# Stick-breaking attention weights turned in 32x32 squares on VectorE and gathered through DRAM

## The chip, the cores and the metric

The kernel runs on one core of one Trainium2 chip. The metric is device time in microseconds (us), the median of a few runs; a profile is one further execution, with its own time. Engines are named as in the profile: PE (TensorE matmul), PEld (its weight load), DVE (VectorE), ACT (ScalarE), POOL (GpSimd) and SP (SyncE, which only issues DMAs here).

## The reference

One decoder layer on 1024 tokens of width 1024, everything in float32:

```python
h = rms_norm(x, norm_gain) * (1 + scale) + shift              # scale, shift, gate from c
q, k, v, z_a, u, z_b, m_a, m_b = split(h @ w_in)              # 8 times 1024 columns
# stick-breaking attention, 16 heads of 64, strictly causal (mask: key < query)
z = q @ k.T * 64 ** -0.5
log_1m_beta = where(mask, -softplus(z), 0)
suffix = cumsum_from_the_right(log_1m_beta) - log_1m_beta
w = where(mask, exp(log_sigmoid(z) + suffix), 0)
attn = w @ v
p_a = (attn * silu(z_a)) @ w_branch_a
p_b = (causal_pooling(u) * silu(z_b)) @ w_branch_b
out = (sigmoid(m_a) * p_a + sigmoid(m_b) * p_b) @ w_out
y = rms_norm(x + gate * out, final_gain)
```

## The kernel before, in words

**Precision.** Operands of the large products are split into a high and a low float32r part, and a product is high*high + high*low + low*high: three matmuls of 128 rows and 512 columns. All matmuls and PE transposes are issued through one helper, so that they have one line, L92, and are told apart by their tiles.

**Stages.** The tokens are reversed on the host, so the causal mask keeps keys that come after the query, and the products of (1 - sigmoid) run from left to right. First come normalisation and the projection u (tiles `ua`, `u`), then v (`v`, stored to DRAM as `v_d`), then the pooling branch (`wzb`, `pool`, `pb`), then attention, and last the branch product (`pa`) and the output product (`o`).

**Attention.** The 16 heads form 8 pairs p of two heads h. Queries are taken in units (p, h, t): t is 0 to 3 and stands for two blocks of 128 queries, qb = 2t and 2t+1. Because of the mask a unit with t = 0 has 1024 and 896 keys, one with t = 3 only 256 and 128. A pair's units come in the order `HT_ORDER`: (h, t) = (0,0), (0,2), (1,0), (1,2), (0,1), (0,3), (1,1), (1,3). For a unit:

- `z_items` (L559 on): PE makes the logits in PSUM, in up to two chunks for a block (tile `z`, two PSUM banks). ACT writes two sigmoids of each chunk, `om` = sigmoid(-z/8) and `be` = sigmoid(z/8) (L576, L577). POOL sets the diagonal block's masked part to 1 and 0 (L581). DVE runs a product scan over `om` (L583) and multiplies `be` by it (L584): `be` is then the weight block, queries on partitions.
- `turn` (L591 on): for a pair kp of key blocks PE transposes up to four 128x128 squares of `be` against `ident` into one PSUM bank (`tr`, two banks); ACT copies the high part (L602, `wt`), DVE the low part (L603).
- `product`: PE multiplies `wt` with the values `vv` of the pair (tile `av`, two banks), and `finish` adds its parts (ACT L626, DVE L628, tile `tp`). After the second head POOL multiplies by the gate silu(z_a), kept in SBUF as `za` (L631), and SP stores the result to `ga_d` (L632).

**Projections as filler.** Between these PE runs the projections of k, q, z_a and of the gates m_a, m_b (tile `p`, two banks `pj`): 40 weight tiles of 16 quanta, a quantum being three 512-column matmuls. `use_k` and `use_q` evict with ACT and DVE (L488, L489; L481, L482), `use_za` with ACT and DVE (L497, L498), the gates with ACT.

**Order.** The attention stage is written as steps, eight to a pair. Step i makes the logits of the unit three places ahead (`LEAD`), turns chunks two ahead (`DEPTH`) of the product, multiplies unit i, and fills up with 70/8 quanta of projection. On PE this order is fixed by hand (`pinned`). The order on ACT, DVE, POOL and SP is chosen by the build's scheduler; each engine then executes its own list strictly in order. SP carries nearly all DMAs, in one queue.

**End.** `load_ga` (L541 on) reads `ga_d` back in 512-column pieces and splits them (ACT L549, DVE L550) into the operand of `pa`.

## Time and profile before

| what | value |
|---|---|
| median of 3 runs | 1249.1 us (1248.1 to 1249.2) |
| profiled execution, its own time | 1250.94 us |
| its span, first to last instruction | 1249.2 us |
| PE busy | 1215.2 us (97%) |
| DVE busy | 810.5 us (65%) |
| ACT busy | 546.3 us (44%) |
| POOL busy | 227.6 us (18%) |
| granted TensorE clock | 0.995 |
| attention stage, about 420 to 1066 us | PE 642.23, DVE 476.04, ACT 374.32 of 646 us |

Busy time is the time in which an engine executes. Every engine is in order, so an instruction that waits holds what is behind it. A line of a group reads: line, engine, operation, out<-in by tile names, shape, count | busy us, mean ns of one | idle time of the engine just before them and what ended it. A line of the timeline reads: start, duration, engine, line, operation, tiles, shape, count, and in brackets the idle time before it.

### The profile page before, as it was taken

The page shows a single profiled execution, that of the slowest core. Times are in us where ns is not written, and L with a number is a line of the kernel's source. Part 1 is how long each engine was busy: PE and PEld are TensorE (multiplying, and loading weights), DVE is VectorE, ACT ScalarE, POOL GpSimd, SP SyncE. Part 2 cuts the span into 40 slices and gives each one's busy share as a digit, 9 for nine tenths or more (in the row PEclk, how much of TensorE's full clock was granted, in tenths as well). Part 3 has the DMA queues.
Part 4 walks back from the last instruction along what each step waited for, and adds up shares of the span by engine and source line. Part 5 has one row for each costly group of instructions (what it writes and reads, how often), then busy time and mean ns, then how long its engine had stood idle before and what let it go on. Part 6 is the DMA issues. An engine that isn't in the chain of part 4 may idle for free.

```text
span 1249.2 us, 16044 instructions
## 1 busy us (share of the span) xinstructions
PE 1215.2 (97%) x5744; PEld 1005.2 (80%) x5744; DVE 810.5 (65%) x1085; ACT 546.3 (44%) x1022; POOL 227.6 (18%) x373
## 2 busy tenths in 40 slices
PE   4999999899999999999999999999999999999998
PEld 3888888688888888888888888888888888888886
DVE  6723452999511168786887877788796864685654
ACT  4654331321111256565566656566565654232101
POOL 2100010111112333221312222132222310001001
PEclk9999999989999999999999999999999999999999
DMA  8649994752344411232322333232233225985612
GB/s 325 265 151 345 320 371 163 274 202 93 118 144 135 151 52 50 69 127 90 105 89 94 114 110 111 73 121 89 89 119 110 74 89 186 352 287 170 201 65 85
DMA packets 72946, 192.97 MB, mean 154 GB/s; under 512 B 7713, under 2 KB 21025, under 8 KB 70946
## 3 DMA queue, kind: packets, MB, share of 16 engines
q1 hardware_dynamic: 62098, 172.80, 40.3%
q10 hardware_dynamic: 10768, 19.14, 4.6%
q8 instruction: 45, 0.74, 0.2%
q14 instruction: 35, 0.29, 0.1%
HBM read 137.38 MB, written 50.34 MB: 150 GB/s over the span
## 4 chain that ended last, share of the span: by engine, by line
PE 78%; DVE 10%; issue 5%; DMA 2%; POOL 1%; ACT 1%; POOLq 0%; SPq 0%; DVEq 0%; ACTq 0%
PE p L92 30%; PE pa L92 7%; PE pb L92 7%; PE v L92 7%; PE o L92 6%; PE av L92 4%; PE z L92 4%; PE u L92 4%; PE wt L92 4%; PE ua L92 2%; DVE om L583 1%; DVE be L584 1%; DMA l_raw<-in_w_in 1%; DVE win L393 1%; PE wzb L92 1%
## 5 line engine op out<-in xcount | busy, mean ns | idle before, releaser
L92 PE MATMUL p<-hT,w 128*128 128x512 f32 x1920 | 534.5, 399 | 0.0
L92 PEld LDWEIGHTS p<-hT,w 128*128 128x128 f32 x1920 | 341.5, 188 | 56.7 <-issue 0.5
L583 DVE TENSOR_TENSOR_SCAN om<-om 128x512 f32<-128x512 f32 (+7 forms) x128 | 175.2, 1368 | 51.7 <-POOL om L581 28.6
L576 ACT ACTIVATE om<-z 128x512 f32<-128x512 f32 (+2 forms) x192 | 94.3, 491 | 104.0 <-PE z L92 101.8
L603 DVE TENSOR_TENSOR wt<-wt,wt 128x512 fp32r<-128x512 f32 (+1 forms) x160 | 101.0, 632 | 47.3 <-ACT wt L602 46.0
L581 POOL TENSOR_SCALAR_AFFINE_SELECT om<-om 128x128 f32<-128x128 f32 x128 | 65.7, 514 | 328.1 <-ACT om L576 301.8
L602 ACT CAST wt<-wt 128x512 fp32r<-128x512 f32 (+1 forms) x160 | 87.3, 546 | 68.7 <-PE wt L92 65.2
L584 DVE TENSOR_TENSOR be<-be,om 128x511 f32<-128x511 f32 (+7 forms) x128 | 99.7, 779 | 10.8 <-ACT wt L602 0.5
L92 PE MATMUL av<-wt,vv 128*128 128x512 f32 x320 | 94.4, 376 | 0.0
L92 PEld LDWEIGHTS wt<-ident,be 128*128 128x128 f32 x576 | 72.0, 140 | 27.5 <-DVE wt L603 3.2
L577 ACT ACTIVATE be<-z 128x512 f32<-128x512 f32 (+2 forms) x192 | 93.6, 487 | 0.0
L92 PE MATMUL wzb<-hT,wzb 128*128 128x512 f32 x384 | 92.9, 398 | 0.1
L92 PE MATMUL wt<-ident,be 128*128 128x128 f32 x576 | 89.2, 273 | 3.8 <-DVE wt L603 3.8
L92 PE MATMUL o<-wo,mhl 128*128 128x512 f32 (+2 forms) x408 | 90.4, 380 | 0.0
L92 PE MATMUL pa<-ga,wa 128*128 128x512 f32 x384 | 89.8, 392 | 0.0
L92 PE MATMUL pb<-gb,wb 128*128 128x512 f32 x384 | 88.1, 391 | 0.0
L92 PEld LDWEIGHTS wzb<-hT,wzb 128*128 128x128 f32 x384 | 73.8, 192 | 16.8 <-DVE zs L411 0.5
L92 PE MATMUL v<-wv,hT 128*128 128x512 f32 x384 | 87.2, 389 | 0.0
L92 PEld LDWEIGHTS o<-wo,mhl 128*128 128x128 f32 x408 | 74.6, 188 | 14.4
L92 PEld LDWEIGHTS pa<-ga,wa 128*128 128x128 f32 x384 | 72.1, 188 | 15.9
L92 PEld LDWEIGHTS pb<-gb,wb 128*128 128x128 f32 x384 | 72.1, 188 | 15.8
L92 PEld LDWEIGHTS v<-wv,hT 128*128 128x128 f32 x384 | 72.1, 188 | 14.9
(121 smaller groups left out, 1458.4 us busy)
## 6 DMA issues: line engine op xcount, KB each, us to landing
w_raw<-in_w_in SPq DMA_DIRECT2D x40, 512.0 KB, 4.3
l_raw<-in_w_in SPq DMA_DIRECT2D x32, 512.0 KB, 5.8
wl_d<-l_raw SPq DMA_DIRECT2D x32, 512.0 KB, 5.3
w<-wl_d SPq DMA_DIRECT2D x32, 512.0 KB, 3.8
v_d<-vo SPq DMA_DIRECT2D x16, 512.0 KB, 5.4
vv<-v_d SPq DMA_DIRECT2D x8, 1024.0 KB, 5.8
wa_raw<-in_w_branch_a SPq DMA_DIRECT2D x16, 512.0 KB, 4.8
wa<-in_w_mod SPq DMA_DIRECT2D x7, 1024.0 KB, 8.7
```

What stands on the lines that cost most here:

```text
L92: ins = op(*args, **kw)
L393: v.tensor_add(nxt[:, :n], cur[:, :n], cur[:, step:step + n])
L576: act.activation(om[:, b0:b0 + n], zp[:, :n], AF.Sigmoid, scale=-0.125)
L577: act.activation(be[:, b0:b0 + n], zp[:, :n], AF.Sigmoid, scale=0.125)
L581: gp.affine_select(out=tl[:, :P], in_=tl[:, :P], pattern=[[1, P]], compare_op=ALU.is_gt, fill=fill, base=0, channel_multiplier=-1)
L583: v.tensor_tensor_scan(om[:, :W], om[:, :W], om[:, :W], 1.0, ALU.mult, ALU.min)
L584: v.tensor_mul(be[:, 1:W], be[:, 1:W], om[:, :W - 1])
L602: act.copy(wt[:, 0, :off], pt[:, :off])
L603: v.tensor_sub(wt[:, 1, :off], pt[:, :off], wt[:, 0, :off].bitcast(F32))
```

## The change

Three things, all in the attention stage and in `load_ga`:

1. **Turning for t = 0.** The 16 units with t = 0 (blocks 0 and 1 of each head) no longer use PE to transpose. After the scan and the multiply, DVE transposes the 32x32 squares inside `be` (for each block two instructions, one for each 512 key columns) and writes them into the tile `om`, whose scan values are used up. SP stores that tile to a DRAM tile `sq_d`, 512 KB for a block, in runs of 512 bytes. When both blocks are stored, SP reads them back in eight loads of 128 KB into two tiles `wm` (each 512 key columns; a load fills 32 partitions), so that keys come to lie on partitions. `take` then splits `wm` into the high part (ACT, L619) and the low part (DVE, L620), and `product` reads its columns in the order in which they now lie. Units with t = 1 to 3 are turned on PE as before.
2. **Gates wait in DRAM.** silu(z_a) is written to `za_d` as soon as it is made, and read back in `load_ga`, where POOL multiplies it in (two loads and one multiply for each 512-column piece). `finish` stores the ungated sum.
3. **Values by head.** `vv` is loaded as two halves, one for each head, in three buffers, in place of one tile for the pair in two buffers.

Buffers change to fit: `om` has three (two before), `tp` two (three before).

```diff
--- before.py
+++ after.py
@@ -71,6 +71,7 @@
     sb_d = dram.tile([KB, P, S], F32, name="sb_d")
     pb_d = dram.tile([KB, P, S], F32, name="pb_d")
     u_d = dram.tile([KB, P, S], F32, name="u_d")
+    za_d = dram.tile([NP, P, S], F32, name="za_d")
     wl_d = dram.tile([5 * KB, P, D], F32, name="wl_d")
 
     ident = const.tile([P, P], F32, name="ident")
@@ -469,7 +470,7 @@
             elif use is use_q:
                 pair[p]["q"] = [tile_(f"q{h}", [S]) for h in range(2)]
             elif use is use_za:
-                pair[p].update(vv=tile_("vv", [8, 2, 2, HD], pl=at), za=tile_("za", [S], F32, at))
+                pair[p]["vv"] = [None, None]
 
         def half(h):
             return slice(64 * h, 64 * h + 64)
@@ -489,13 +490,15 @@
                 v.tensor_sub(kl[r, h, sl], ps[r], kh[r, h, sl].bitcast(F32))
                 act.dma_start(kh[o, h, sl].bitcast(F32), kh[r, h, sl].bitcast(F32))
 
-        def load_v(p):
-            nc.sync.dma_start(pair[p]["vv"].rearrange("p b h i d -> p (b h i d)").bitcast(F32), v_d[p].rearrange("p b c -> p (b c)"))
+        def load_v(p, h):
+            vv = pair[p]["vv"][h] = at.tile([P, 8, 2 * HD], F32R, tag="vv", bufs=3, name=f"vv{p}_{h}")
+            nc.sync.dma_start(vv.bitcast(F32), v_d[p][:, :, 2 * HD * h:2 * HD * (h + 1)])
 
         def use_za(p, sh, ps):
-            z = pair[p]["za"][:, sh * 512:sh * 512 + 512]
+            z = at.tile([P, 512], F32, tag="sg", bufs=3, name=f"za{p}_{sh}")
             act.activation(z, ps, AF.Sigmoid)
             v.tensor_mul(z, ps, z)
+            nc.sync.dma_start(za_d[p][:, sh * 512:sh * 512 + 512], z)
 
         def projections():
 
@@ -519,7 +522,9 @@
                 load(i + 1)
                 pair_tiles(p, use)
                 if use is use_za:
-                    load_v(p)
+                    load_v(p, 0)
+                    if p == 0:
+                        load_v(p, 1)
                 gate = use not in (use_k, use_q, use_za)
                 if gate:
                     out_ = sigmoid_out(at, 3, use[p], f"m{ct}")
@@ -542,9 +547,12 @@
             ga = []
             for p in ps:
                 r_ = fing.tile([P, 512], F32, tag="gr", bufs=3, name=f"gr{sh}_{p}")
-                ins = (act if sh == 0 else nc.sync).dma_start(r_, ga_d[p][:, sh * 512:sh * 512 + 512])
-                if sh == 1:
-                    tc.keep_in_program_order(ins)
+                z_ = fing.tile([P, 512], F32, tag="zr", bufs=3, name=f"zr{sh}_{p}")
+                for t_, d_ in ((r_, ga_d), (z_, za_d)):
+                    ins = (act if sh == 0 else nc.sync).dma_start(t_, d_[p][:, sh * 512:sh * 512 + 512])
+                    if sh == 1:
+                        tc.keep_in_program_order(ins)
+                gp.tensor_mul(r_, r_, z_)
                 g_ = fing.tile([P, 2, 512], F32R, tag="ga", bufs=12, name=f"ga{sh}_{p}")
                 act.copy(g_[:, 0], r_)
                 v.tensor_sub(g_[:, 1], r_, g_[:, 0].bitcast(F32))
@@ -559,10 +567,12 @@
             p, h, t = u
             st = pair[p]
             rows = unit_rows[u] = []
+            if t == 0:
+                sq_d = dram.tile([P, 2, 4, 2, P], F32, tag="sq_d", bufs=3, name=f"sq_d{p}_{h}")
             for qb in (2 * t, 2 * t + 1):
                 n0 = qb * P
                 W = S - n0
-                om = atz.tile([P, S], F32, tag="om", bufs=2, name=f"om{p}_{h}_{qb}")
+                om = atz.tile([P, S], F32, tag="om", bufs=3, name=f"om{p}_{h}_{qb}")
                 g = t // 2
                 be = at.tile([P, S - 512 * g], F32, tag=f"be{g}", bufs=NBE[g], name=f"be{p}_{h}_{qb}")
                 nch = (W + 511) // 512
@@ -582,12 +592,40 @@
                     if i == nch - 1:
                         v.tensor_tensor_scan(om[:, :W], om[:, :W], om[:, :W], 1.0, ALU.mult, ALU.min)
                         v.tensor_mul(be[:, 1:W], be[:, 1:W], om[:, :W - 1])
-                        rows.append(be)
+                        if t > 0:
+                            rows.append(be)
+                        else:
+
+                            for f, (b0, c0) in enumerate(((qb, 0), (0, 512 - n0))):
+                                tq = om[:, f * 512:f * 512 + 512].rearrange("p (j b c) -> p b j c", j=4, c=32)[:, b0:]
+                                v.transpose(tq, be[:, c0:512 * (f + 1) - n0].rearrange("p (b j c) -> p b j c", j=4, c=32))
+                            nc.sync.dma_start(sq_d[:, :, :, qb].rearrange("p f j n -> p (f j) n"), om.rearrange("p (g n) -> p g n", n=P))
                     yield
+            if t == 0:
+
+                for f in range(2):
+                    wm = at.tile([P, 4, 2, P], F32, tag="wm", bufs=3, name=f"wm{p}_{h}_{f}")
+                    for j in range(4):
+                        src = sq_d[:, f, j].rearrange("(i k) r n -> k i (r n)", k=32)
+                        nc.sync.dma_start(wm[32 * j:32 * j + 32].rearrange("k i r n -> k i (r n)"), src)
+                    rows.append(wm)
+
+        def take(u, kp):
+
+            p, h, t = u
+            src = unit_rows[u][kp // 2][:, :, :, 64 * (kp % 2):64 * (kp % 2) + 64].rearrange("p i r n -> p r i n")
+            wt = at.tile([P, 2, 512], F32R, tag="wt", bufs=NWT, name=f"wt{p}_{h}_{t}_{kp}")
+            hi, lo = (wt[:, i].rearrange("p (r i n) -> p r i n", r=2, i=4) for i in range(2))
+            act.copy(hi, src)
+            v.tensor_sub(lo, src, hi.bitcast(F32))
+
+            return wt, [(1, 32, 8), (0, 0, 4)] if kp == 0 else [(2 * kp, 0, 8), (2 * kp + 1, 32, 8)]
 
         def turn(u, kp):
 
             p, h, t = u
+            if t == 0:
+                return take(u, kp)
             rows, k0 = unit_rows[u], 2 * t
             pt = bank("tr", f"wt{p}_{h}_{t}_{kp}")
             blocks, off = [], 0
@@ -606,12 +644,17 @@
         def product(u, kp, wt, blocks):
 
             p, h, t = u
-            vv = pair[p]["vv"]
+            vv = pair[p]["vv"][h]
             if kp == t:
                 avs[u] = bank("av", f"av{p}_{h}_{t}").rearrange("p (a q) -> p a q", a=2)
             for j, (kb, o, n) in enumerate(blocks):
+                if t == 0:
+                    mov = wt.rearrange("p a (g n) -> p a g n", n=64)[:, :, :n, o:o + 32]
+                    n *= 32
+                else:
+                    mov = wt[:, :, o:o + n]
                 mm(
-                    avs[u][:, :, :n], vv[:, kb, h].rearrange("p a d -> p (a d)"), wt[:, :, o:o + n],
+                    avs[u][:, :, :n], vv[:, kb], mov,
                     start=kp == t and j == 0, stop=kp == 3 and j == 1,
                 )
 
@@ -621,15 +664,16 @@
             del unit_rows[u]
             av, r = avs.pop(u), half(h)
             if h == 0:
-                both[t] = at.tile([P, 256], F32, tag="tp", bufs=3, name=f"tp{p}_{t}")
+                both[t] = at.tile([P, 256], F32, tag="tp", bufs=2, name=f"tp{p}_{t}")
             tp = both[t]
             act.copy(tp[r], av[64:128, 0])
             for i in range(2):
                 v.tensor_add(tp[r], av[0:64, i], tp[r])
             if h == 1:
                 sl = slice(t * 256, t * 256 + 256)
-                gp.tensor_mul(tp, tp, pair[p]["za"][:, sl])
                 nc.sync.dma_start(ga_d[p][:, sl], tp)
+            if (h, t) == (0, 3) and p + 1 < NP:
+                load_v(p + 1, 1)
             if (h, t) == HT_ORDER[-1]:
                 del pair[p]
```

Counted over the program: PE has 240 transposes of 128x128 fewer (336 are left of 576). DVE has 64 transposes of squares more; 64 of its 160 `wt` splits now read `wm`, all at 512 columns (16 of them had 384). SP issues 32 stores to `sq_d`, 128 loads of `wm`, 16 stores to `za_d`, 16 loads of `vv` in place of 8, and 8 loads of `zr`; ACT issues 8 more loads of `zr`. POOL has 32 multiplies of 128x256 fewer and 16 of 128x512 more.

How the order moves is shown at the turn from pair 2 to pair 3 (667 to 700 us of the profile before): the unit (h, t) = (0, 0) of pair 3, whose logits are made two to three steps ahead of its product. In the rows a name carries head, block and chunk (`z_1_0_1` is head 1, block 0, second chunk; `wt_0_0_2` is head 0, t 0, kp 2), and its last number is only the buffer's; lines are those of each kernel's own file.

On PE, at the logits of the next unit (1, 0), before:

```order
L92 MATMUL z_1_0_0_5533<-kh_4768,q_3_4953 128x512
L92 MATMUL z_1_0_0_5533<-kl_2956,q_3_4953 128x512
L92 MATMUL p_0_5473<-hT,w_16_5304 128x512 x3
L92 MATMUL wt_0_0_1_5551<-ident,be_0_0_5355 128x128
L92 MATMUL wt_0_0_1_5551<-ident,be_0_1_5396 128x128
L92 MATMUL wt_0_0_1_5551<-ident,be_0_0_5355 128x128
L92 MATMUL wt_0_0_1_5551<-ident,be_0_1_5396 128x128
L92 MATMUL p_1_5559<-hT,w_16_5304 128x512 x6
```

and now:

```order
L93 MATMUL z_1_0_0_5545<-kh_4782,q_3_4968 128x512
L93 MATMUL z_1_0_0_5545<-kl_2957,q_3_4968 128x512
L93 MATMUL p_0_5489<-hT,w_16_5298 128x512 x3
L93 MATMUL p_1_5566<-hT,w_16_5298 128x512 x6
L93 MATMUL z_1_0_1_5573<-kh_4782,q_3_4968 128x512
L93 MATMUL z_1_0_1_5573<-kl_2957,q_3_4968 128x512
```

The four transposes of `wt_0_0_1` are gone, and the projection `p` runs on; the other PE work stands in the old order.

On ACT at the same place, before:

```order
L602 CAST wt_0_0_0_5512<-wt_0_0_0_5508 128x384
L626 COPY tp_1_5347<-av_1_1_5464 64x256
L576 ACTIVATE om_1_0_5531<-z_1_0_0_5533 128x512
L577 ACTIVATE be_1_0_5532<-z_1_0_0_5533 128x512
L488 CAST kh_5472<-p_0_5473 64x512
L602 CAST wt_0_0_1_5556<-wt_0_0_1_5551 128x512
L490 DMA kh_5472<-kh_5472 64x512
L488 CAST kh_5472<-p_0_5473 64x512
L576 ACTIVATE om_1_0_5531<-z_1_0_1_5566 128x512
L577 ACTIVATE be_1_0_5532<-z_1_0_1_5566 128x512
```

and now:

```order
L669 COPY tp_1_5340<-av_1_1_5480 64x256
L586 ACTIVATE om_1_0_5543<-z_1_0_0_5545 128x512
L587 ACTIVATE be_1_0_5544<-z_1_0_0_5545 128x512
L489 CAST kh_5488<-p_0_5489 64x512
L491 DMA kh_5488<-kh_5488 64x512
L619 CAST wt_0_0_0_5524<-wm_0_0_5439 128x512
L489 CAST kh_5488<-p_0_5489 64x512
L619 CAST wt_0_0_1_5563<-wm_0_0_5439 128x512
L586 ACTIVATE om_1_0_5543<-z_1_0_1_5573 128x512
L587 ACTIVATE be_1_0_5544<-z_1_0_1_5573 128x512
```

The first split of the unit stood ahead of the sigmoids of `z_1_0_0`; now it stands behind them, and the sigmoids of `z_1_0_1` behind two splits, both of which read `wm`.

On DVE a little earlier, from the weights of block 1 of that unit on, before:

```order
L584 TENSOR_TENSOR be_0_1_5396<-be_0_1_5396,om_0_1_5395 128x895
L603 TENSOR_TENSOR wt_1_1_3_5440<-wt_1_1_3_5435,wt_1_1_3_5440 128x512
L583 SCALAR_TENSOR_TENSOR om_0_4_5446<-om_0_4_5446 128x512
L498 TENSOR_TENSOR za_5308<-p_1_5391,za_5308 128x512
L584 TENSOR_TENSOR be_0_4_5447<-be_0_4_5447,om_0_4_5446 128x511
L603 TENSOR_TENSOR wt_1_3_3_5481<-wt_1_3_3_5477,wt_1_3_3_5481 128x384
L583 SCALAR_TENSOR_TENSOR om_0_5_5492<-om_0_5_5492 128x384
L603 TENSOR_TENSOR wt_0_0_0_5512<-wt_0_0_0_5508,wt_0_0_0_5512 128x384
L584 TENSOR_TENSOR be_0_5_5493<-be_0_5_5493,om_0_5_5492 128x383
L628 TENSOR_TENSOR tp_1_5347<-av_1_1_5464,tp_1_5347 64x256 x2
L489 TENSOR_TENSOR kl_2955<-p_0_5473,kh_5472 64x512
L603 TENSOR_TENSOR wt_0_0_1_5556<-wt_0_0_1_5551,wt_0_0_1_5556 128x512
```

and now:

```order
L594 TENSOR_TENSOR be_0_1_5395<-be_0_1_5395,om_0_1_5394 128x895
L593 SCALAR_TENSOR_TENSOR om_0_4_5460<-om_0_4_5460 128x512
L601 STREAM_TRANSPOSE om_0_1_5394<-be_0_1_5395 128x3x4x32
L601 STREAM_TRANSPOSE om_0_1_5394<-be_0_1_5395 128x4x4x32
L500 TENSOR_TENSOR za_1_5476<-p_1_5390,za_1_5476 128x512
L594 TENSOR_TENSOR be_0_4_5461<-be_0_4_5461,om_0_4_5460 128x511
L641 TENSOR_TENSOR wt_1_3_3_5497<-wt_1_3_3_5493,wt_1_3_3_5497 128x384
L593 SCALAR_TENSOR_TENSOR om_0_5_5508<-om_0_5_5508 128x384
L594 TENSOR_TENSOR be_0_5_5509<-be_0_5_5509,om_0_5_5508 128x383
L671 TENSOR_TENSOR tp_1_5340<-av_1_1_5480,tp_1_5340 64x256 x2
L490 TENSOR_TENSOR kl_2956<-p_0_5489,kh_5488 64x512
L620 TENSOR_TENSOR wt_0_0_0_5524<-wm_0_0_5439,wt_0_0_0_5524 128x512
```

The scan reads SCALAR_TENSOR_TENSOR here. The squares of block 1 are transposed behind the scan of the next unit's block (`om_0_4`), and seven rows of other work (eight instructions) stand between them and the first split that reads the gathered tile.

## The prediction

> **What bounds the kernel now.** I read the page first (busy time, then the chain of waits), then busy time by stage, then the timeline of one turn from pair to pair.
>
> ```profile
> span 1249.2 us, 16044 instructions
> PE 1215.2 (97%) x5744; PEld 1005.2 (80%) x5744; DVE 810.5 (65%) x1085; ACT 546.3 (44%) x1022; POOL 227.6 (18%) x373
> PE 78%; DVE 10%; issue 5%; DMA 2%; POOL 1%; ACT 1%; POOLq 0%; SPq 0%; DVEq 0%; ACTq 0%
> ```
>
> PE is busy almost throughout and makes up 78% of the chain that ended last. The stages, from the view of busy time in stretches (PE, PEld, DVE, ACT, POOL, then clock, DMA share, GB/s):
>
> ```profile
> 420.00:1066.00 646.00, 642.23 (x3201) 533.97 (x3200) 476.04 (x634) 374.32 (x766) 164.31 (x299) 1.00 0.32 102
> 667.00:742.00 75.00, 74.52 (x376) 61.79 (x375) 59.05 (x79) 45.32 (x95) 19.06 (x36) 1.00 0.29 95
> 1066.00:1118.00 52.00, 52.00 (x229) 42.60 (x228) 37.84 (x50) 16.92 (x17) 0.00 (x0) 1.00 0.91 327
> ```
>
> In the attention stage PE works 642 of 646 us and DVE 476 (74%). So work taken from PE there shortens the stage, as long as no other engine's wait takes its place. DVE has 16 us to spare in the 75 us of a pair, but not evenly:
>
> ```profile
> 682.00:692.00 10.00, 10.00 (x51) 8.32 (x49) 8.40 (x8) 7.73 (x16) 4.13 (x6) 1.00 0.50 161
> 692.00:702.00 10.00, 9.52 (x50) 7.51 (x49) 9.66 (x14) 5.89 (x13) 2.74 (x7) 1.00 0.41 129
> ```
>
> From 682 to 702 us, the turn to the next pair, DVE works 18.1 of 20 us.
>
> **What PE sheds.** The matmuls of a group overlap, so I price a group of transposes by the time from its start to the next start (timeline of PE):
>
> ```profile
> 671.51 0.60 PE L92 MATMUL wt<-ident,be 128*128 128x128 f32 x4
> 671.86 0.95 PE L92 MATMUL p<-hT,w 128*128 128x512 f32 x3
> 674.85 0.49 PE L92 MATMUL wt<-ident,be 128*128 128x128 f32 x3
> 675.09 0.94 PE L92 MATMUL p<-hT,w 128*128 128x512 f32 x3
> ```
>
> Four transposes take 0.35 us, three 0.24. The change removes, in each of 16 units, three groups of four and one of three: 48 x 0.35 + 16 x 0.24 = 20.6 us. The group's mean of 273 ns would give 65 us for 240 of them; that counts the overlap twice, so I don't use it.
>
> ```profile
> L92 PE MATMUL wt<-ident,be 128*128 128x128 f32 x576 | 89.2, 273 | 3.8 <-DVE wt L603 3.8
> ```
>
> PE also waited 3.8 us in all ahead of transposes, until DVE had emptied a `tr` bank. The units with t = 0 leave those banks, so between 0 and 3.8 goes; I take 2. Gain: **22.6 us**, 2.8 for each of the 8 pairs.
>
> **What DVE gets.** No transpose of squares stands in the trace. The nearest groups:
>
> ```profile
> L116 DVE CAST mhl<-m 128x512 fp32r<-128x512 f32 x16 | 6.8, 423 | 0.3
> L603 DVE TENSOR_TENSOR wt<-wt,wt 128x512 fp32r<-128x512 f32 x96 | 65.8, 685 | 25.4 <-ACT wt L602 24.6
> L603 DVE TENSOR_TENSOR wt<-wt,wt 128x384 fp32r<-128x384 f32 x64 | 35.3, 551 | 21.8 <-ACT wt L602 21.4
> L583 DVE TENSOR_TENSOR_SCAN om<-om 128x512 f32<-128x512 f32 x16 | 19.5, 1217 | 0.3 <-POOL om L581 0.3
> ```
>
> A cast of 512 columns takes 0.42 us, a subtraction 0.69, a scan 1.22. A transpose has one source, like the cast, but writes in another order; I take the subtraction's price, one element after the other. 48 of 512 columns and 16 of 384: 48 x 0.685 + 16 x 0.551 = 41.7 us; by the cast (three quarters of it for 384) 25, by the scan 73. The 16 splits that grow from 384 to 512 columns add 16 x 0.134 = 2.1. That is 5.5 us a pair: DVE at about 64.5 of then 72 us. On average it fits. [...]
>
> **The new wait.** The gathered tile must be ready when ACT reaches the first split. I follow the unit (0,0) of pair 3 on the timeline of before.
>
> ```profile
> 671.56 2.00 DVE L583 TENSOR_TENSOR_SCAN om<-om 128x896 f32<-128x896 f32 x1
> 673.69 1.09 DVE L584 TENSOR_TENSOR be<-be,om 128x895 f32<-128x895 f32 x1
> 675.30 1.22 DVE L583 TENSOR_TENSOR_SCAN om<-om 128x512 f32<-128x512 f32 x1
> 681.58 0.60 ACT L576 ACTIVATE om<-z 128x512 f32<-128x512 f32 x1 [1.47 <-PE z L92]
> 682.08 0.59 ACT L577 ACTIVATE be<-z 128x512 f32<-128x512 f32 x1
> 682.55 0.57 ACT L488 CAST kh<-p 64x512 fp32r<-64x512 f32 x1
> 687.94 0.34 PE L92 MATMUL z<-kh,q 128*128 128x384 f32 x1
> ```
>
> DVE: two transposes of block 0 come ahead of the scan at 671.56, so it starts near 672.9. Then, in the new order, scan 2.0, a split 0.69, the multiply 1.09, the next scan 1.22, transposes 0.55 + 0.69: done at about 679.2. Now SP stores 512 KB and, once that has landed, issues four loads of 128 KB for the first tile.
>
> ```profile
> v_d<-vo SPq DMA_DIRECT2D x16, 512.0 KB, 5.4
> kh<-kh ACTq DMA_DIRECT2D x32, 128.0 KB, 3.0
> ga_d<-tp SPq DMA_DIRECT2D x32, 128.0 KB, 1.8
> L632 SPq DMA_DIRECT2D ga_d<-tp x32: 319/320/326, 499.1 to 1056.9; - x32
> DMA to landing us min/median/max: 2.9/5.6/9.6
> DMA to landing us min/median/max: 1.7/2.2/6.0
> ```
>
> These are rows of the view of DMA issues (size, median from issue to landing) and of the views of the tiles `v_d` and `ga_d`, stores and loads together. A 512 KB store has a median of 5.4 us, and the shortest on `v_d` is 2.9. For 128 KB: 1.7 (shortest on `ga_d`, last row) to 3.0. An issue takes 0.32, so the fourth goes 0.96 after the first. The store's runs are shorter than any in these rows, but less else is moving (DMA share 0.50): I take 3.9 and 2.6. The tile is there at 679.2 + 3.9 + 0.96 + 2.6 = **686.7**; bounds 684.8 and 688.8.
>
> ACT is ready for it at 682.55 + 0.57 less 0.24 (a group of three transposes gone before that point) = 682.9, and waits 3.8 us (1.9 to 5.9). Behind the waiting split on ACT stand a copy of `kh`, the second split and the two sigmoids of `z_1_0_1`. At their spacing of 0.5 us these five end 2.6 after the tile lands: 689.3. Only then is that PSUM bank free for the fourth chunk of logits, which PE wants at 687.94 less 0.59 (a second group gone) = 687.35. PE stalls 2.0 us (0.1 to 4.1): **16 us** over 8 pairs (1 to 33). The unit (1,0) has a whole step more between logits and first split, 9.3 us by 75/8, which is above the worst of these waits: 0.
>
> On SP, behind the waiting load, stand `ga_d<-tp`, a half of the values and the next weights; in the trace that weight load (`w<-wl_d`) follows the store of `tp` and isn't yet due: two tiles are loaded ahead, and one lasts 16 x 0.69 = 11 us of PE alone. SP's hold, 3.9 + 8 x 0.32 = 6.5 us, is covered; without that cover PE would lose it at each pair. [...]
>
> **What is late next.** DVE's first split can't run before ACT's, 687.3; where it had 1.9 us to spare between 682 and 702, it now loses about 3 waiting and has 2.5 of transposes of unit (1,0) more. It comes out 3.6 us late.
>
> ```profile
> 695.76 0.69 DVE L489 TENSOR_TENSOR kl<-p,kh 64x512 fp32r<-64x512 f32 x1
> 700.49 0.58 ACT L481 CAST q<-p 64x512 fp32r<-64x512 f32 x1 [0.32 <-PE p L92]
> ```
>
> The first to feel it is the `pj` bank that `kl` frees at 696.45 and PE refills at 700.4, when the first half of q is done: 3.9 us of slack, a little less with PE running ahead. I put 0.4 a pair: **3 us** (0 to 12).
>
> **The rest.** `load_ga` gets a multiply on POOL and twice the loads; `finish` loses one.
>
> ```profile
> L631 POOL TENSOR_TENSOR tp<-tp,za 128x256 f32<-128x256 f32 x32 | 30.4, 952 | 115.9 <-DVE tp L628 115.9
> L785 POOL TENSOR_TENSOR y<-y,fg 128x512 f32<-128x512 f32 x1 | 1.3, 1292 | 0.1
> ```
>
> At the last piece of `ga` 1.29 comes in and 0.95 goes: 0.3. Half of the gates, 2 MB, are read where DMAs are at 0.91 and 327 GB/s: 6.4 us of DMA time, but PE works 52.00 of 52 there and the operand is for the second half. I take 1 (0 to 6). The stores of gates and the halves of values move no byte more on the path: 16 + 8 issues of 0.32 on a queue that mostly waits; 0.
>
> **Sum.** -22.6 + 16 + 3 + 1 = -2.6 us. The profiled execution took 1250.9 us (span 1249.2); -2.6 gives 1248.3. The runs' median lies 1.8 below the profiled time: **1246 us**. Favourable ends give -24.4 + 1 = -23, unfavourable -20.6 + 33 + 12 + 6 = +30.
>
> **The rivals.**
> - *Hidden gather, 1228.* If store and loads land at their shortest, 684.8, PE's stall is 0.1 and the gain stays: -22.6 + 1 + 1 = -21. For it: DMA share is only 0.3 in the stage. Against: that needs the minima of both rows at once.
> - *ACT held by the gather, 1264, slower.* With 5.6 and 3.0 the tile lands at 688.8, PE stalls 4.1 x 8 = 33 and DVE lateness grows with it: -22.6 + 33 + 4 + 1 = +15. The point from which it decides: 2.8 us gain a pair less 0.5 leaves 2.3, so a landing later than about 687.0, 7.8 us behind the last transpose. For it: the medians in a busy stretch. Against: SP's own stores of 128 KB land at 1.8.
> - *DVE becomes the bound, 1263, slower.* At the scan's price a transpose costs 0.53 more: 8 a pair, four of them in the full stretch, 2.1 x 8 = 17 on top of the forecast. For it: a scattered write. Against: the cast at 0.42.
> - That PE keeps its transposes is excluded: the order has 336 of 576.
>
> **How the numbers follow.** Forecast 0.40 (own range 1238 to 1252), hidden gather 0.22, ACT held 0.23, DVE bound 0.15. A measurement tells about 0.2%, 2.5 us, from no change. Faster: 0.23 of the forecast's share and all of the hidden gather, 0.45; same: 0.13 of the forecast's and 0.02 of the rest, 0.15; slower 0.40. The range that leaves out 2 in 10 runs from the hidden gather to a little above the slower rivals: 1228 to 1267.
>
> **What would show it.** Right: PE's `wt` group at 336, PE busy about 20 us less; waits of ACT at the first split (L619) for the loads of `wm`, 2 to 6 us eight times, none for unit (1,0); PE waits on ACT's sigmoids of `z` or on `kl` of about 2 to 3 us a pair; transposes near 0.69 us. Wrong: no wait at L619 (hidden gather), transposes above 1 us, waits of PE for weights, or a stall behind `load_ga`.

## The result, and the profile after

The changed kernel takes **1304.0 us** (median of 4 runs, 1302.1 to 1306.7) against 1248.8 of the kernel before: a ratio of 1.045 (95% interval 1.0437 to 1.0462), 55 us slower. Forecast were 1246 us, in a range of 1228 to 1267. The profiled execution took 1306.7 us.

The page of the changed kernel: span, busy time, the chain that ended last by engine and by line.

```profile
span 1305.0 us, 16028 instructions
PE 1219.9 (93%) x5504; PEld 1000.7 (77%) x5504; DVE 848.3 (65%) x1149; ACT 545.7 (42%) x1022; POOL 232.9 (18%) x357
PE 71%; DVE 8%; issue 8%; DMA 6%; ACT 2%; POOL 1%; SPq 1%; ACTq 0%; POOLq 0%; DVEq 0%
```

PE has 240 instructions fewer and is busy 4.7 us *longer*, and its share of the chain falls from 78 to 71%, while DMA rises from 2 to 6%. So two things want an explanation: idle time of PE, and busy time that grew although work was taken away. The attention stage, from the first matmul of `p` to the first of `pa`, as one stretch (PE, PEld, DVE, ACT, POOL, clock, DMA share, GB/s):

```profile
417.30:1121.00 703.70, 645.87 (x2963) 528.22 (x2962) 510.32 (x699) 374.29 (x767) 159.38 (x275) 0.96 0.50 150
```

It is 57 us longer than the 646.7 us before: the whole loss lies here. DVE works 510 of 704 us, so over the whole stage it isn't full. The clock is 0.96 where it was 1.00. The list of waits says who waited for whom (total us, times, longest):

```profile
ACT wt L619 <- DMA wm<-sq_d: 66.2, 24, 6.0
DVE wt L620 <- ACT wt L619: 45.7, 14, 6.4
PE av L93 <- issue: 25.8, 7, 5.8
PE z L93 <- ACT be L587: 19.7, 9, 3.6
PE p L93 <- DVE kl L490: 5.5, 5, 2.4
PE av L93 <- DVE wt L620: 4.1, 2, 3.2
```

ACT waits at the split for the gathered tile, DVE behind ACT, and PE behind both: 19.7 us at logits whose bank the sigmoid behind the split has to empty, and 25.8 + 4.1 us at the products of the split tile ("issue" names no releaser; these products start 0.1 us after DVE has ended the low part, 653.31 against 653.21 in the case below). In all PE idles 57.8 us in the stage, where before it idled 3.8.

The costliest kind, unit (1,0) of pair 2, on the timeline (SP, then DVE, ACT, PE):

```profile
641.43 0.52 SPq L602 DMA_DIRECT2D sq_d<-om  x1
644.95 3.65 SPq L610 DMA_DIRECT2D wm<-sq_d  x8
...
640.20 1.16 DVE L601 STREAM_TRANSPOSE om<-be 128x384 f32<-128x384 f32 x2
652.53 2.48 DVE L620 TENSOR_TENSOR wt<-wm,wt 128x512 fp32r<-128x512 f32 x4
...
649.80 1.14 ACT L619 CAST wt<-wm 128x512 fp32r<-128x512 f32 x2 [0.31 <-DMA wm<-sq_d]
...
639.23 0.85 PE L93 MATMUL p<-hT,w 128*128 128x512 f32 x3
639.93 0.33 PE L93 MATMUL z<-kh,q 128*128 128x384 f32 x1
...
646.86 1.53 PE L93 MATMUL p<-hT,w 128*128 128x512 f32 x6
653.31 0.98 PE L93 MATMUL av<-wt,vv 128*128 128x512 f32 x2 [4.91 <-issue]
654.09 1.48 PE L93 MATMUL p<-hT,w 128*128 128x512 f32 x3
655.37 0.41 PE L93 MATMUL z<-kh,q 128*128 128x256 f32 x1
```

The last transposes end at 641.4, the store is issued at once, the first load 3.5 us later, eight loads take 3.65 us to be issued, and ACT has the first half at 649.8, 8.4 us behind the transposes. DVE, in order, comes to the low parts only at 652.5. In this pair 2.1 us of that are rows of DVE's own that still stand ahead of the low part when ACT's first split has ended (650.4); in the other seven pairs it is 0 to 1.0 us. PE has had nothing to do since 648.4. And then three matmuls of `p` take 655.37 - 654.09 = 1.28 us from start to start, where at 639.23 three took 0.70. The stretches around it:

```profile
640.00:648.40 8.40, 8.39 (x40) 6.77 (x38) 8.17 (x13) 4.67 (x12) 3.26 (x4) 1.00 0.75 208
648.40:650.50 2.10, 0.00 (x0) 0.00 (x0) 2.07 (x3) 1.28 (x3) 0.00 (x0) 0.99 0.95 223
650.50:657.30 6.80, 3.99 (x11) 3.35 (x12) 4.94 (x9) 2.23 (x5) 0.56 (x2) 0.50 0.06 13
```

From 650.5 to 657.3 the granted clock is 0.50. The stage holds 61.4 us of such stretches, each 3.4 or 6.8 us long; before it had none. Outside them a matmul of 512 columns starts 231 ns (median) after the one before, inside them 427. Summed over all instructions of the stage against their own kind outside, the half clock costs **25.0 us** by itself (other ways to form this sum give 23 to 26).

So the stage's balance is -20.6 (transposes) - 3.8 (idle time of before) + 57.8 (idle time now) + 25.0 (half clock) = +58.4, against +57.0 measured.

### The profile page after: what moved, and what is told of

Same layout as the page of the kernel before. It is cut to its first block, busy times and chain, and to the rows that moved or that the text cites. A ratio compares the mean times of both kernels' runs of the same rounds, so it can differ in the third digit from the quotient of the medians.

```text
span 1305.0 us, 16028 instructions
## 1 busy us (share of the span) xinstructions
PE 1219.9 (93%) x5504; PEld 1000.7 (77%) x5504; DVE 848.3 (65%) x1149; ACT 545.7 (42%) x1022; POOL 232.9 (18%) x357
## 3 DMA queue, kind: packets, MB, share of 16 engines
q1 hardware_dynamic: 132754, 212.66, 49.9%
## 4 chain that ended last, share of the span: by engine, by line
PE 71%; DVE 8%; issue 8%; DMA 6%; ACT 2%; POOL 1%; SPq 1%; ACTq 0%; POOLq 0%; DVEq 0%
PE p L93 23%; PE pa L93 7%; PE pb L93 7%; PE v L93 7%; PE o L93 6%; PE wzb L93 5%; PE u L93 4%; PE av L93 4%; PE z L93 3%; DVE om L593 2%; PE ua L93 2%; PE wt L93 2%; DMA sq_d<-om 2%; DMA wm<-sq_d 2%; PE pool L93 1%
## 5 line engine op out<-in xcount | busy, mean ns | idle before, releaser
L93 PE MATMUL p<-hT,w 128*128 128x512 f32 x1920 | 541.7, 408 | 8.3 <-DVE kl L490 5.5
L93 PEld LDWEIGHTS p<-hT,w 128*128 128x128 f32 x1920 | 357.2, 195 | 76.0 <-issue 6.4
L591 POOL TENSOR_SCALAR_AFFINE_SELECT om<-om 128x128 f32<-128x128 f32 x128 | 81.6, 638 | 485.0 <-ACT om L586 459.2
L93 PE MATMUL av<-wt,vv 128*128 128x512 f32 x320 | 98.5, 390 | 29.9 <-issue 25.8
L93 PEld LDWEIGHTS av<-wt,vv 128*128 128x128 f32 x320 | 62.1, 199 | 46.7 <-issue 28.6
L93 PEld LDWEIGHTS wzb<-hT,wzb 128*128 128x128 f32 x384 | 74.0, 193 | 16.4
L93 PE MATMUL z<-kh,q 128*128 128x512 f32 (+2 forms) x192 | 67.0, 349 | 19.7 <-ACT be L587 19.7
L641 DVE TENSOR_TENSOR wt<-wt,wt 128x384 fp32r<-128x384 f32 (+1 forms) x96 | 59.1, 616 | 40.0 <-ACT wt L640 39.2
L640 ACT CAST wt<-wt 128x384 fp32r<-128x384 f32 (+1 forms) x96 | 51.3, 535 | 56.9 <-PE wt L93 49.8
```

Source lines behind the costliest of these rows:

```text
L93: ins = op(*args, **kw)
L591: gp.affine_select(out=tl[:, :P], in_=tl[:, :P], pattern=[[1, P]], compare_op=ALU.is_gt, fill=fill, base=0, channel_multiplier=-1)
L640: act.copy(wt[:, 0, :off], pt[:, :off])
L641: v.tensor_sub(wt[:, 1, :off], pt[:, :off], wt[:, 0, :off].bitcast(F32))
```

## The experiments

Theory G: the gathered tile comes late, ACT and DVE stand in their fixed order at its split, and PE behind them; each stall can bring a stretch at half clock. Rivals: DVE is too full of transposes; the added DMA traffic; the other two parts of the change. In the table idle time and half clock are those of the stage, summed from each trace as above; ratios are against the kernel before on the same chip.

| kernel | us | ratio (95%) | stage | PE idle | at half clock | its cost |
|---|---|---|---|---|---|---|
| before | 1248.8 | | 646.7 | 3.8 | 0 | 0 |
| changed | 1304.0 | 1.045 (1.044 to 1.046) | 703.7 | 57.8 | 61.4 | 25.0 |
| turning undone | 1250.0 | 1.0017 (1.0008 to 1.0027) | 648.7 | 5.4 | 0 | 0 |
| no wait for the gather | 1240.2 | 0.994 (0.992 to 0.995) | 638.9 | 16.4 | 3.4 | 1.7 |
| only (0,0) | 1266.6 | 1.015 (1.013 to 1.017) | 664.3 | 26.7 | 10.2 | 4.8 |
| only (1,0) | 1278.1 | 1.024 (1.022 to 1.026) | 674.5 | 32.5 | 20.5 | 8.5 |
| fillers | 1315.7 | 1.055 (1.053 to 1.058) | 714.8 | 39.3 | 20.5 | 9.3 |
| four steps | 1256.1 | 1.006 (1.004 to 1.008) | 655.6 | 28.2 | 20.5 | 8.4 |
| four steps, low part on POOL | 1257.6 | 1.008 (1.006 to 1.009) | 656.0 | 29.6 | 13.7 | 6.3 |
| before, four steps | 1246.7 | 0.999 (0.998 to 1.000) | 645.2 | 1.8 | 3.4 | 1.6 |
| four steps, split late | 1265.4 | 1.013 (1.012 to 1.015) | 662.8 | 33.9 | 23.9 | 11.2 |
| four steps, split held | 1247.3 | 0.999 (0.998 to 1.000) | 645.7 | 22.3 | 13.7 | 5.3 |
| three steps, split late | 1311.4 | 1.050 (1.049 to 1.052) | 708.5 | 64.5 | 54.6 | 21.4 |
| before, long gaps | 1295.6 | 1.039 (1.037 to 1.040) | 693.6 | 34.8 | 23.9 | 10.8 |
| before, short gaps | 1349.9 | 1.082 (1.080 to 1.084) | 749.3 | 68.3 | 41.0 | 19.1 |
| four steps, held, first pair on PE | 1240.7 | 0.994 (0.992 to 0.995) | 639.1 | 14.9 | 10.2 | 3.6 |
| the same, four loads | 1249.4 | 1.001 (1.000 to 1.002) | 646.8 | 20.3 | 13.7 | 4.8 |

### Turning undone

```diff
+def T0(u):
+    return False
...
-            if t == 0:
+            if T0(u):
                 return take(u, kp)
```

(and the same at the four other places that ask for t = 0)

> The changed kernel with the turning alone undone: units with t = 0 are transposed on PE again, so no squares on VectorE, no store to the DRAM tile and no gather; gates in DRAM, values by head and the buffer counts stay as changed. Theory G (the gathered tile comes late, ACT and DVE stand at its split, and PE's clock halves after each of PE's stalls): the whole loss sits in the turning, so this comes back to the kernel before, 1249 +- 4 us, with idle PE of about 4 us in the attention stage and no stretch at half clock. Rival R (the other two parts, or the buffer counts, cost a good part of it): 1260 or more.

1250.0 us, no half clock. Gates in DRAM, values by head and the buffer counts cost 2 us (0.17%); the other 53 come from turning in squares.

### No wait for the gather

```diff
-                        src = sq_d[:, f, j].rearrange("(i k) r n -> k i (r n)", k=32)
+                        src = first[0][:, f, j].rearrange("(i k) r n -> k i (r n)", k=32)
```

(`first[0]` is the first unit's DRAM tile, which gets its own buffer)

> The changed kernel with its squares, stores, eight loads a unit and splits all in place, but every unit's loads read the DRAM tile that the very first unit stored, so that none of them waits for its own unit's transposes and store (from the second unit on the attention weights of t = 0 are those of the first; timing only). All of the DVE work and all of the DMA traffic stay. Theory G (late gather): the waits of ACT and DVE at the split vanish, PE idles under 10 us in the stage, no half clock, and the shed transposes show as a gain: 1228 us (1222 to 1236). Rival D (DVE is late by its added 33 us of transposes whatever the gather does): 1270 or more, DVE as the releaser of PE's waits. Rival T (DMA traffic or SP's queue of loads): 1290 or more, as changed.

1240.2 us, above the 1222 to 1236 that were expected. DVE has every transpose still (849.4 us busy against 848.3), the DMAs are all there (212.66 MB on the largest queue in both), and the waits of the changed kernel are gone but for the first unit. The waits of PE in it:

```profile
PE p L93 <- DVE kl L490: 6.1, 6, 2.7
PE z L93 <- ACT be L589: 4.1, 3, 2.8
PE p L93 <- ACT m_sg L179: 3.3, 2, 2.7
PE p L93 <- DVE q L483: 2.8, 5, 1.7
```

That rules out both rivals as the cause: with the same DVE load and the same DMA traffic, 64 us of the loss are gone. (The loads go out earlier, from the second unit on mostly 55 to 60 us ahead of the unit's own last store, so a clash of just these bursts isn't excluded by this run; the runs with four steps below, whose gathers do wait, speak against it.) The 12 us by which it missed 1228 are in these waits: 8.9 us are PE behind DVE (`kl`, `q`), which may be what the transposes cost when nothing else is late; no run tests that by itself. The stage gains 7.8 us: the shed 20.6 less 12.7 more of idle time and 1.7 of half clock is 6.2, so 1.6 stay unexplained.

### One unit alone

```diff
 def T0(u):
-    return False
+    return u[1:] == (0, 0)
```

and `(1, 0)` in the other run.

> Turned in squares only for the unit (0,0) of each pair; (1,0) is transposed on PE as before. Theory G: PE sheds half, 10 us, and keeps the stalls at the logits, 17 us of gaps in the changed profile, with about half of the half-clock loss of some 24 us: 1249 - 10 + 17 + 12 = 1268 (1258 to 1278). Rival D (lateness of DVE adds up over both units, neither alone reaches PE): 1240 to 1252.

> Turned in squares only for the unit (1,0) of each pair; (0,0) is transposed on PE as before. The prediction put this unit's wait at nothing: then PE sheds 10 us and the time is 1239. Theory G, by the gaps ahead of this unit's products in the changed profile (30 us) and half of the half-clock loss: 1249 - 10 + 30 + 12 = 1281 (1268 to 1290). Rival D2 (this unit is late only because (0,0)'s wait, transposes and splits have made DVE late ahead of it): 1237 to 1245.

1266.6 and 1278.1, both as theory G had it. Each unit is late by itself; (1,0), which the prediction put at nothing, is the dearer one. The balances close: 664.3 - 646.7 = 17.6 against -10.3 + 22.9 + 4.8 = 17.4, and 27.8 against -10.3 + 28.7 + 8.5 = 26.9. In the run with (1,0) alone the stall reaches PE by another door as well (lines are four higher there):

```profile
PE wt L97 <- DVE wt L645: 12.4, 10, 3.7
PE z L97 <- ACT be L591: 9.4, 5, 3.2
PE av L97 <- issue: 4.6, 1, 4.6
```

DVE, standing at the low part of the gathered tile, doesn't empty the `tr` banks of the units that PE still turns.

### Fillers

```diff
+        def keep_busy(bk):
+            for _ in range(12):
+                mm(bk, h_hi[:, 0, :P], h_hi[:, 0, :512], start=True, stop=True)
...
+                if (h, t) == (1, 0):
+                    keep_busy(bk)
```

(and once more ahead of the fourth chunk of logits of (1,0), into the bank of the next product)

> The changed kernel with 12 idle-time matmuls of 512 columns (12 x 0.229 = 2.75 us, results overwritten) put on PE at the two places of each pair where it stands still: ahead of the fourth chunk of logits of unit (1,0), and ahead of the first product of unit (1,0). They add 16 x 2.75 = 44 us of PE work and take nothing away; ACT and DVE wait as before. Theory G with the clock: the 57 us of gaps shrink by nearly as much as is added (overshoot where a gap was shorter: by the list of gaps some 8 us), and PE no longer falls to half clock, which saves most of the 24 us: 1304 - 24 + 8 = 1288 (1280 to 1296), faster although it does more. Rival (half clock is only a mark beside the gaps and costs nothing, or comes from something else than PE's idling): 1304 + 8 = 1312 (1306 to 1325).

1315.7: the number is the rival's, and yet the rival's reason is not what the trace shows. The 192 matmuls add 44 us, the idle time falls by only 18.5 (PE's waits at logits rise from 9 to 14, 24.2 us), since holding PE back also makes the next logits later; the half clock's cost falls from 25.0 to 9.3. 44 - 18.5 - 15.7 = +9.8 against +11.1 measured in the stage. As a test of the clock it failed: it moved the stalls.

### Four steps ahead, on both kernels, and with POOL

```diff
-LEAD = {0: 3, 1: 3, 2: 3, 3: 3}
+LEAD = {0: 4, 1: 4, 2: 4, 3: 4}
```

> The changed kernel with one number changed for all units: logits four steps ahead of the product, not three, so that store and gather get about 9 us more. Everything else as changed, nothing left out. Theory G: the waits at the split go (they were at most 6.6 us), and what is left is what the run without the wait left: 1240 us (1235 to 1245), under the kernel before. Rival D (DVE too full whenever squares are turned): 1265 or more. Rival B (the buffers of weight blocks and of gathered tiles, whose number is the same, now hold DVE or SP a step longer): 1250 to 1290, with waits on be, wm or weights in the list.

> Control: the kernel before with logits four steps ahead. Nothing in it waits for a gather, so the extra step buys nothing: 1248 (1245 to 1252). If it falls to 1240 as well, the gain of the changed kernel with four steps isn't the gather's.

```diff
-            v.tensor_sub(lo, src, hi.bitcast(F32))
+            gp.tensor_sub(lo, src, hi.bitcast(F32))
```

> Four steps ahead, and the low part of the t = 0 splits (64 subtractions of 512 columns) made on POOL in place of DVE. It takes 64 x 0.69 = 44 us from DVE, more than the 32 us that the squares brought. If the rest of DVE's lateness (8 us of PE waiting for kl and q in the run without the wait) is what still stands between 1240 and the full gain of 20.6 us: 1232 (1228 to 1236). Rival: POOL takes about 1.3 us for each and holds the masks of the next logits behind it, or slows DVE beside it: 1242 or more.

Four steps take 48 us off the changed kernel, and 1.3 off the one before. But 1256 is not the 1240 of theory G: ACT still waits for the tile (42.6 us in all, 13 times). ACT's list in the run with four steps, then the product that the split is for:

```profile
539.96 1.14 ACT L619 CAST wt<-wm 128x512 fp32r<-128x512 f32 x2 [5.08 <-DMA wm<-sq_d]
541.00 0.59 ACT L586 ACTIVATE om<-z 128x512 f32<-128x512 f32 x1
...
542.13 0.50 PE L93 MATMUL z<-kh,q 128*128 128x512 f32 x1 [1.95 <-ACT be L587]
...
553.06 0.52 PE L93 MATMUL av<-wt,vv 128*128 128x512 f32 x2
```

ACT stands 5.1 us at a split whose product runs 13 us later, and the sigmoids behind it hold PE 1.95. The scheduler that makes ACT's list has put the split that early; by what reckoning, the traces don't show. With the low part on POOL (1302 ns there, 684 on DVE) the time is the same, 1257.6: PE's waits behind `kl` fall from 10.9 to 6.7 us, those at logits rise from 14.8 to 20.3, and to take the low part from DVE wins nothing here.

### Where the split stands in ACT's list

```diff
-            act.copy(hi, src)
+            tc.keep_in_program_order(act.copy(hi, src))
```

holds the split behind whatever ACT was given before it in the program ("split held"). "Split late" besides writes it one chunk ahead of its product in place of two:

```diff
+        def take_now(c):
+            if c < len(chunks) and chunks[c][0][2] == 0 and turned_[c] is None:
+                turned_[c] = turn(*chunks[c])
...
+                for k in range(c, c + 2):
+                    take_now(k)
```

> Logits four steps ahead, and the splits of t = 0 written one chunk ahead of their product (two before) and held to that place in ACT's list. In the run with four steps ACT stood at the split 2 to 6.5 us although the product wanted it only 10 to 13 us later: the order put the split early in ACT's list. Theory P (the place of the split in ACT's list, and not the latency of the gather, makes PE wait once there are four steps): ACT's waits for wm under 1 us, PE's waits at logits gone, 1240 us (1234 to 1245). Rival D (what is left at four steps is DVE's fullness, seen as kl and q late): 1250 to 1258, as with four steps alone.

> Logits four steps ahead, and the splits only held to the place in ACT's list where they are written (two chunks ahead of their product; for unit (0,0) that is over a step ahead, since the step between has one chunk). Theory P: the splits of the second to fourth chunk move back, the first of (0,0) hardly does, so its waits stay in part: 1248 (1242 to 1254), between the run with four steps and the one with the later place. Rival D: 1250 to 1258 for both.

> Three steps as changed, splits one chunk ahead of their product and held there. Theory P with latency: for unit (0,0), whose product came 4 to 6.6 us after the split, the wait moves behind the fourth chunk of logits and stops costing; for (1,0), whose product waits for the tile itself (split to product 1.4 to 2.3 us), nothing is won: 1304 - 17 - 12 = 1275 (1262 to 1287). Rival (the wait only moves from the logits to the product): 1298 to 1310.

The order of the three is not what I expected. Held in its place, the split waits 8.7 us in all (five times), and the time is 1247.3, even with the kernel before. One chunk later is worse, 1265.4 where theory P had 1240: ACT hardly waits (2.5 us in all), but DVE's low part now comes behind other work and PE waits for it. In the longest case (6.7 us) the low part stands behind a `kl` for which DVE itself waits 4.3 us on ACT.

```profile
PE av L93 <- DVE wt L620: 28.2, 9, 6.7
```

With three steps the later split wins nothing either (1311.4): its wait moves from the logits to the product, as the rival said (a little above its 1298 to 1310). So theory P holds in one half only: too early a place makes ACT stand, too late a place makes PE stand, and with four steps there is room between the two.

### Idle time put into the kernel before

```diff
+        def gap(bk):
+            mm(bk[:, :128], gt[:, :128], gt[:, :128], start=True, stop=True)
+            for _ in range(1):
+                gp.tensor_scalar(gt[:, :896], gt[:, :896].bitcast(F32), 1.0, 0.0, op0=ALU.mult, op1=ALU.add)
+            mm(bk[:, :128], gt[:, :128], gt[:, :128], start=True, stop=True)
...
+                if t == 0:
+                    gap(bk)
```

(short gaps: 256 columns, and `t < 3`)

> The kernel before (no squares, no gather) with 16 long gaps put into PE's order: ahead of the first product of each unit with t = 0 stand two 128x128 matmuls, and the second waits for a POOL instruction of 896 columns that starts when the first has ended (about 2.2 us by the 2.5 us of POOL's rows of 1024 columns; with the hand-overs some 2.5). Nothing else waits. Theory C (a gap of this length brings a stretch at half clock that costs time of its own, up to 1.7 us for 3.4 us): 1249 + 40 of idle time + up to 16 x 1.7 = 1316 (1300 to 1320), with several stretches at 0.50 in the stage. Rival (half clock costs nothing): 1289 (1284 to 1294).

> The same with 48 short gaps: at the first product of every unit with t below 3, the POOL instruction has 256 columns (0.65 us, with the hand-overs some 0.95). About the same idle time, 46 us. Theory C: gaps under 1 us do not halve the clock, so the time is 1249 + 46 = 1295 and the loss equals the added idle time. Rival: the same time; but then the run with long gaps also loses no more than its idle time.

The long gaps in the list of waits:

```profile
PE av L92 <- POOL gt L563: 34.8, 16, 3.9
```

and one of them on PE's timeline:

```profile
547.46 0.42 PE L92 MATMUL av<-gt 128*128 128x128 f32 x1 [2.50 <-POOL gt L563]
547.68 0.95 PE L92 MATMUL av<-wt,vv 128*128 128x512 f32 x2
548.42 1.48 PE L92 MATMUL p<-hT,w 128*128 128x512 f32 x3
```

Nothing but PE's order was changed here, and three matmuls of `p` take 1.28 us after the gap as in the changed kernel. The stage is 46.9 us longer: 31.1 of added idle time, 10.8 of half clock, and 5.0 left for the 32 added matmuls (0.16 each). So the half clock follows PE's own idling and costs time of its own; without it the run would have been at 1285. The total, 1295.6, lies below my 1300 to 1320, since only six of the 16 gaps brought a stretch. The short gaps were not short: POOL's instructions stood behind the masks of the logits, and 23 of 48 gaps were over 1.5 us. So that run (1349.9 in place of 1295) is no control; its balance is of the same kind (64.5 idle + 19.1 half clock, 19 us for 96 matmuls).

### A version under both kernels

```diff
+def T0(u):
+    return u[2] == 0 and u[0] > 0
```

on top of four steps and the held split: the first pair, whose logits can't be made earlier, stays on PE.

> The run with four steps and the splits held to their place, with the first pair's units turned on PE as before (its logits have no lead to give; 9.5 us of gaps stood there). 14 of 16 units stay turned in squares. Theory P: -9.5 - 3 for half clock + 2.6 for the transposes that return = 1237 (1233 to 1242), under the kernel before. Rival (PE's waits only move on to the next pair): 1245 to 1250.

1240.7 us, ratio 0.9936 (0.9921 to 0.995): 7.5 us under the kernel before and 63 under the changed one, near the 1237 of theory P. From its page:

```profile
PE 1196.2 (96%) x5534; PEld 987.8 (80%) x5534; DVE 843.8 (68%) x1141; ACT 542.3 (44%) x1022; POOL 231.0 (19%) x357
```

and from its list of waits (lines four higher) what still holds PE:

```profile
PE p L97 <- DVE kl L494: 6.9, 4, 2.8
PE av L97 <- DVE wt L624: 6.0, 2, 5.5
```

PE is busy 19 us less than before. What is left of idle time is DVE's lateness at `kl` and one product.

### Four loads for a unit

```diff
-                sq_d = dram.tile([P, 2, 4, 2, P], F32, tag="sq_d", bufs=3, name=f"sq_d{p}_{h}")
+                sq_d = dram.tile([4, 2, P, 2, P], F32, tag="sq_d", bufs=3, name=f"sq_d{p}_{h}")
...
+                    src = sq_d[j].rearrange("f (i k) r n -> k (f i) (r n)", k=32)
```

(`wm` one tile of double size, `NWT` 3)

> As the run with the first pair on PE, and a unit's gather in four loads of 256 KB in place of eight of 128 KB (the columns are written and stored in another order, one gathered tile of double size for a unit, three split tiles in place of four to make room). If the number of loads holds SP and the tiles (at one pair eight loads took 9.2 us to be issued, and the splits waited 4.8 and 1.5 us): 2 to 6 us less, 1233 (1229 to 1238). Rival (the loads are no longer on the path; three split tiles hold DVE): 1237 to 1250.

1249.4, 8.6 us slower than with eight, at the slow end of the rival's range. By the code each load now carries a part of both halves, so the first split waits for all four, and ACT's waits for the tile rise to 26.8 us (9 times) from 6.6 (5 times), with loads that land after 6.2 us (median) in place of 4.6. Three split tiles in place of four may have their part in it; the run doesn't separate the two.

## Why the prediction was wrong

**What PE sheds: right.** 336 transposes are left, the 3.8 us of waits at the `tr` banks are gone altogether (2 were put), and the run without the wait shows the 20.6 us in its balance.

**What DVE gets: right.** 0.685 and 0.551 us were put for a transpose:

```profile
L601 DVE STREAM_TRANSPOSE om<-be 128x512 f32<-128x512 f32 x48 | 31.2, 674 | 0.1
L601 DVE STREAM_TRANSPOSE om<-be 128x384 f32<-128x384 f32 x16 | 8.9, 557 | 0.0
```

The DVE-bound rival, which needed the scan's price, is out.

**The gather of unit (0,0): mechanism right, length short.** The last transposes end 8.4 us (mean) after the last logits; 679.2 less 670.3, 8.9, was put. From there to the split 7.5 us were put (3.9 + 0.96 + 2.6), and 8.9 were measured: the store took less, 3.5, but loads go out 0.47 us apart in place of 0.32 and land after 3.7 in place of 2.6. That is beyond the 7.8 from which, by the prediction's own words, the rival "ACT held by the gather" decides; its 1264 is still 40 us short. ACT waits 4.4 us (3.8 put), and PE's idle time for this unit is 18.8 us at the logits and 0.9 at a product, against 16.

**The unit (1,0): the step that failed.** "A whole step more between logits and first split, 9.3 us" was taken from the number of steps, and not from rows. In the trace of before the first split of (0,0) of pair 3 starts 8.3 us after its last logits (ending at 670.28), and that of (1,0) 13.4 us after (688.46):

```profile
669.94 0.34 PE L92 MATMUL z<-kl,q 128*128 128x384 f32 x1
...
678.59 0.48 ACT L602 CAST wt<-wt 128x384 fp32r<-128x384 f32 x1 [0.15 <-PE wt L92]
...
688.12 0.34 PE L92 MATMUL z<-kl,q 128*128 128x384 f32 x1
...
701.85 0.48 ACT L602 CAST wt<-wt 128x384 fp32r<-128x384 f32 x1
```

So it has 5 us more, and not 9. Even the prediction's own figures would have warned: it put 16.4 us from the last logits of (0,0) to the gathered tile (686.7 less 670.3), and (1,0) has 13.4. And the 5 us are gone before the gather begins: DVE ends the transposes of (1,0) 13.8 us after its logits (8.4 for (0,0)). With 8.9 for the gather the split is due at 22.7 where the order of before had it at 13.4. Only a part of this comes from standing behind the waits of (0,0): the transposes of (1,0) still end 11.2 us after the logits in the run without the wait, where no gather holds DVE, and 9.8 in the run with (1,0) alone, where the split begins 19.7 us after the logits and the kernel takes 1278. How far the rest is the added transposes and how far the list's order, no run separates. I had DVE "3.6 us late" at this very place and led it on to the `pj` bank, but not to this unit's own transposes. The cost is 29.0 us of idle PE where 0 stood.

**Half clock: a term that was not there.** 25.0 us. The granted clock of before was 1.00 in the stage, and nothing in the prediction asked what happens to it when PE stands still for 2 to 6 us.

**What is late next, and the rest.** `kl` holds PE 5.5 us (3 put, bounds 0 to 12); 2.7 us at gates at the end of the stage, and 2 us for the other two parts (1 put). SP's hold was covered, as put: no wait of PE for weights is in the list.

Put together: a forecast of -2.6 with 16 for (0,0), and what the trace shows in its place is 19.7 for (0,0), 29.0 for (1,0) and 25.0 of half clock. The two last terms are the miss.

Store and loads added up, as the sum had it: in the changed kernel a unit's first load is issued 3.5 us (median of 16; 3.5 to 4.3) after its second store.

## What to carry to other kernels

When work moves from a busy engine to a path through DMAs, count for *every* user of that path, in rows of the trace, how long its input has before the order wants it; here 8.3 and 13.4 us against some 17 and 22. A fixed list on an idle engine makes such a wait everybody's: give it more lead and hold the waiting instruction at its place in the list, neither as early as the scheduler likes nor as late as the product allows. And price a stall of PE above its length when it nears 2 us, since the matmuls after it may run at half clock (here after 13 of 75 gaps of 1 to 2 us, and after 26 of 57 of 2 to 3).

## What the runs showed of the hardware

**PE's clock was halved after short stalls.** Over the 17 profiles, PE's gaps in the attention stage by length, and how many had a stretch at 0.50 begin in them or within 3.4 us behind:

| gap, us | gaps | with half clock |
|---|---|---|
| 0.4 to 1 | 86 | 0 |
| 1 to 2 | 75 | 13 |
| 2 to 3 | 57 | 26 |
| 3 and more | 43 | 40 |

The changed kernel alone has 0 of 6, 1 of 4, 4 of 7 and 7 of 7. Six of its stretches last 3.4 us and six 6.8, and in them a 512-column matmul takes 427 ns in place of 231 (median, start to start). The length of a gap alone doesn't settle it: in the changed kernel a gap of 2.59 us that ends at 465.52 brought a stretch, and one of 2.52 that ends at 490.65 none. So it is in the run with long gaps, too. Beside the gap of 2.50 us shown above, after which three matmuls of `p` take 1.28 us, stands this one, after which they take 0.69:

```profile
869.10 0.33 PE L92 MATMUL av<-gt 128*128 128x128 f32 x1 [2.51 <-POOL gt L563]
869.67 0.85 PE L92 MATMUL p<-hT,w 128*128 128x512 f32 x3
870.36 0.39 PE L92 MATMUL z<-kh,q 128*128 128x512 f32 x1
```

**Loads of 128 KB that are issued in a row** go out 0.47 us apart in the changed kernel and land after 3.7 us (medians; 2.5 to 6.4 to landing), where SP's stores of the same size land after 2.2 in the same profile. In the run with four steps and the split held, the eight loads of one unit took 9.2 us to be issued, behind loads of weights and values:

```profile
746.16 0.66 SPq L149 DMA_DIRECT2D w<-wl_d  x1
746.92 1.10 SPq L495 DMA_DIRECT2D vv<-v_d  x1
...
749.77 9.22 SPq L610 DMA_DIRECT2D wm<-sq_d  x8
```
